# Two weight sums of a seven-product feed-forward step, moved from VectorE to accumulating DMA

## Chip, core and metric

The kernel runs on one core of a Trainium2 chip. The metric is the device time of one execution in microseconds (us); lower is better. Three runs of the kernel before gave 1428.53, 1428.57 and 1429.28 us, median 1428.57 us. A separate profiled execution gives the trace that is read below.

## What is computed

A two-layer hybrid block on 512 tokens of width 1024: layer 0 mixes tokens with dilated window attention, layer 1 with an mLSTM, and each is followed by a gated feed-forward block; a root-mean-square norm ends it. All data are 32-bit floats. Only the input half of the feed-forward block is changed:

```python
D_FF = -(-8 * D_MODEL // (3 * 256)) * 256        # 2816
def swiglu(xn, w_in, w_out):
    gu = xn @ w_in                                # 1024 x 5632
    return (jax.nn.silu(gu[..., :D_FF]) * gu[..., D_FF:]) @ w_out
```

The first 2816 columns of `gu` are called gates here, the last 2816 ups.

## The kernel before

Every matrix product is made of three TensorE passes: an operand is split into a rounded high part and the rest (`hi`, made by ScalarE on L208; `lo`, made by VectorE on L209), and high times high, high times low and low times high are summed in PSUM. `ffn_in` (L859) makes the hidden activations of a layer in pairs of 128 columns, j = 0, 2, ... 20. The pairs 0, 2 and 4 are made plainly (`plain`, L943). The eight pairs j = 6 to 20 are each made as one **step of seven products**: weights and tokens are seen as 2 x 2 blocks. A11 and A12 are the blocks of the gate columns for the upper and the lower 512 input features, A21 and A22 those of the up columns, each 512 x 256 numbers (512 KB, a tile of 128 x 1024). B11 to B22 are blocks of the normalized tokens. Sums of blocks are multiplied, seven products in place of eight (`PRODUCTS`, L855): p1 = A11 B11, p5 = S1 T1, p6 = S2 T2, p2 = A12 B21, p7 = S3 T3, p3 = S4 B22, p4 = A22 T4, in this order on TensorE.

The token sums T1 to T4 and their splits are made once a layer, while the plain pairs run (`normalized`, L893). The weight sums are made in every step, by VectorE on L988:

- S1 = A21 + A22, S2 = S1 - A11 (both in one tile, tag `t1`, of which there is one: the next step's S1 cannot be written before this step's S2 has been read for the last time, by S4);
- S3 = A11 - A21 (in place of A21, in the tile pair `w8`, of which there are two), S4 = A12 - S2 (in place of A12).

`weights_of` (L970) issues the four loads of a step on SyncE's queue (SP): A11 and A21 into one `w8` pair, A22 and A12 into tiles of the ring `wraw` (three). `prepare` (L992) splits one operand and then makes the sum that follows it; it runs two products ahead of TensorE (`AHEAD`, L857), because `hi` and `lo` are rings of three tiles (`W_BUFS`). So S1 of the next step is split while p4 of the present step runs, and S4 of the present step is made about when its p6 begins. `products` (L1005) issues the 24 matmuls of a product (L1017) and the evaluation: L1023 adds, L1055 the silu, L1056 and L1060 the products gate times up that give the two token halves of the hidden tile.

Each engine works through its instructions in program order; an engine that waits holds up all that is behind it. The loads of a step are issued as soon as their tile is free and the queue has come to them. GpSimd (POOL) issues no DMA in this stage of the kernel before.

Of the kernel before, what the change touches and what calls it, by code (L numbers as in the profile page):

```python
# [11 lines left out]
F32 = mybir.dt.float32  # L12
# [3 lines left out]
ALU = mybir.AluOpType  # L16
AX = mybir.AxisListType
P = 128
# [52 lines left out]
def tile_hybrid_dilated_attn_mlstm(  # L71
# [4 lines left out]
    nc = tc.nc  # L76
# [268 lines left out]
    with ExitStack() as actx:  # L345
# [16 lines left out]
        ang, n, sn, cs = (tmp[:, 0, i * P:(i + 1) * P] for i in range(4))  # L362
# [430 lines left out]
        def out_project(pairs, w2d, nk, name, first=0, end=KC // 2):  # L793
            for c in range(first, end):
# [4 lines left out]
        acc = [[acc_tile("awo0_%d" % m) for m in range(2)],  # L799
               [ps.tile([P, 512], F32, tag="s", name="awo1_%d" % m, bufs=2) for m in range(2)],  # L800
               [acc_tile("awo2_0"), ps.tile([P, 512], F32, tag="t", name="awo2_1", bufs=1)]]
# [51 lines left out]
    HALF = SEQ // 2  # L853
# [5 lines left out]
    def ffn_in(layer, fp, pair, rbc, hook, following):  # L859
# [4 lines left out]
        wi = ffn_w_in[layer]  # L864
# [20 lines left out]
        ops, raw = {}, {}  # L885
# [7 lines left out]
        def normalized():  # L893
            xs = [fp.tile([P, 4, SEQ], F32, tag="w8", name="f%dx%d" % (layer, i), bufs=2) for i in range(2)]
            for i in range(2):
                for t in range(2):
                    raw["B%d%d" % (i + 1, t + 1)] = xs[i][:, :, t * HALF:(t + 1) * HALF]
            for k in range(KC):
                nc.vector.scalar_tensor_tensor(xs[k // 4][:, k % 4], h[k], col("ffn", layer * KC + k), rbc,
                                               op0=ALU.mult, op1=ALU.mult)  # L900
                yield
            split_tokens("B11")
            raw["T1"] = fp.tile([P, 4, HALF], F32, tag="t1", name="f%dt1" % layer)
            nc.vector.tensor_tensor(raw["T1"], raw["B12"], raw["B11"], op=ALU.subtract)
            yield

            raw["T3"] = raw["B12"]
            nc.vector.tensor_tensor(raw["T3"], raw["B22"], raw["B12"], op=ALU.subtract)
            split_tokens("T1")
            yield  # L910
            split_tokens("T3")
            yield
            split_tokens("B22")
            yield
            raw["T2"] = raw["B22"]
            nc.vector.tensor_tensor(raw["T2"], raw["B22"], raw["T1"], op=ALU.subtract)
            split_tokens("T2")
            yield
            split_tokens("B21")
            yield  # L920

            raw["T4"] = raw["B21"]
            nc.vector.tensor_tensor(raw["T4"], raw["B21"], raw["T2"], op=ALU.subtract)
            split_tokens("T4")

        hid = []
# [43 lines left out]
        def weights_of(j):  # L970

            nm = "f%dj%d" % (layer, j)
            w8 = fp.tile([P, 2, 1024], F32, tag="w8", name=nm + "_w8", bufs=2)
            w = {"A11": w8[:, 0], "A21": w8[:, 1]}
            for key in ("A22", "A12"):
                w[key] = wp.tile([P, 1024], F32, tag="wraw", name=nm + key, bufs=W_BUFS)
            for key in ("A11", "A22", "A12", "A21"):
                half, ch = int(key[1]) - 1, int(key[2]) - 1
                c0 = half * D_FF + j * P
                nc.sync.dma_start(w[key].rearrange("p (k n) -> p k n", k=4),  # L980
                                  wi[ch * 4 * P:(ch + 1) * 4 * P, c0:c0 + 256].rearrange("(k p) n -> p k n", p=P))

            def split(key):
                return split_chunk((w[key], 1024, lambda t: t.rearrange("p (k n) -> p k n", k=4), nm + key))

            def total(key, a, b, op, place):
                w[key] = w[place]
                nc.vector.tensor_tensor(w[key], w[a], w[b], op=op)  # L988
            w["own"] = fp.tile([P, 1024], F32, tag="t1", name=nm + "S")
            made = {}  # L990

            def prepare(key):  # L992
                made[key] = split(key)

                if key == "A11":
                    total("S1", "A21", "A22", ALU.add, "own")
                elif key == "S1":
                    total("S2", "S1", "A11", ALU.subtract, "own")
                elif key == "S2":
                    total("S3", "A11", "A21", ALU.subtract, "A21")  # L1000
                elif key == "A12":
                    total("S4", "A12", "S2", ALU.subtract, "A12")
            return [(lambda key=key: prepare(key)) for key, _ in PRODUCTS], made

        def products(j, made):  # L1005
            nm = "f%dj%d" % (layer, j)
            acc, t = {}, {}
            first = lambda x: x.rearrange("p (m n) -> p m n", m=2)

            def product(key, okey, name, fresh=True):  # L1010
                if fresh:
                    acc[name] = bank("%s_%s" % (nm, name))
                whl = made[key]
                for m in range(2):
                    for k in range(4):
                        for a, b in SPLITS:
                            nc.tensor.matmul(acc[name][:, m * HALF:(m + 1) * HALF], whl[a][:, k, m * P:(m + 1) * P],  # L1017
                                             ops[okey][b][:, k],
                                             start=(fresh and m == 0 and k == 0 and (a, b) == SPLITS[0]),
                                             stop=(m == 1 and k == 3 and (a, b) == SPLITS[-1]), skip_group_check=True)  # L1020

            def add(out, x, y, op=ALU.add):
                nc.vector.tensor_tensor(out, x, y, op=op)  # L1023


            def p1():
                product("A11", "B11", "c11")
                acc["u"] = bank(nm + "_u")
                nc.scalar.activation(acc["u"], acc["c11"], AF.Copy)

            def p5():
                product("S1", "T1", "p5")
                t["v5"] = temp("v5", nm + "v5")
                nc.scalar.activation(t["v5"], acc["p5"], AF.Copy)

            def p6():
                product("S2", "T2", "u", fresh=False)
                t["u2"] = temp("u2", nm + "u2")
                nc.scalar.activation(t["u2"], acc["u"], AF.Copy)

            def p2():
                product("A12", "B21", "c11", fresh=False)
                t["g1"] = temp("gu0", nm + "g1", 3)
                nc.scalar.activation(t["g1"], acc["c11"], AF.Silu)

            def p7():
                product("S3", "T3", "u", fresh=False)
                add(t["v5"], acc["u"], t["v5"])

            def p3():  # L1050
                product("S4", "B22", "p5", fresh=False)
                hid.append(hidden(j // 2))
                t["g2"] = temp("gu0", nm + "g2", 3)
                add(t["g2"], acc["p5"], t["u2"])
                nc.scalar.activation(t["g2"], t["g2"], AF.Silu)  # L1055
                nc.vector.tensor_tensor(hid[-1][:, :, HALF:], first(t["v5"]), first(t["g2"]), op=ALU.mult)  # L1056

            def p4():
                product("A22", "T4", "u", fresh=False)
                nc.vector.tensor_tensor(hid[-1][:, :, :HALF], first(acc["u"]), first(t["g1"]), op=ALU.mult)  # L1060
            return [p1, p5, p6, p2, p7, p3, p4]

        split_next()
# [44 lines left out]
    with ExitStack() as fctx:  # L1108
        fp = pool(fctx, "ffn0")
        a, ready = ffn_in(0, fp, pair, rbc, hook,  # L1110
                          lambda ch: split_chunk(weight_chunk(ffn_w_out[0], ch, 0, 4, "fo0_k%d" % ch)))
# [17 lines left out]
    with ExitStack() as mctx:  # L1129
# [101 lines left out]
        for b in range(TB):  # L1231
            ve.scalar_tensor_tensor(fblk[32 * b:32 * b + H], blk(lf)[:, b], bias2[:, 1:2], blk(t0)[:, b],
                                    op0=ALU.add, op1=ALU.add)
# [174 lines left out]
    with ExitStack() as fctx:  # L1408
        fp = pool(fctx, "ffn1")
        wo = ffn_w_out[1]  # L1410

        def load(ch, n):
            src = wo[ch * 2 * P:(ch + 1) * 2 * P, n * 512:(n + 1) * 512].rearrange("(k p) n -> p k n", p=P)
            return split_weights(src, [P, 2, 512], "fw%d_%d" % (n, ch))
        a, ready = ffn_in(1, fp, pair, rbc, hook, lambda ch: load(ch, 0))
# [40 lines left out]
        for n in range(2):  # L1456
            acc = ([acc_tile("fin%d" % i) for i in range(3)] + [ps.tile([P, 512], F32, tag="t", name="fin3", bufs=1)]
                   if n == 0 else
                   [ps.tile([P, 512], F32, tag=tg, name="fin4", bufs=2) for tg in ("s", "s", "o", "o")]
                   + [acc_tile("fin5")])  # L1460
# [23 lines left out]
            for at, tb, cs in tiles:  # L1484
# [4 lines left out]
                t = ts[tb, n][:, cs]  # L1489
# [7 lines left out]
                if part == (1 if tb == TB - 1 else 0):  # L1497
                    nc.vector.tensor_tensor(fpre[:, tb:tb + 1], fss[:, tb, 0:1], fss[:, tb, 1:2], op=ALU.add)
                    nc.vector.tensor_scalar(fpre[:, tb:tb + 1], fpre[:, tb:tb + 1], 1.0 / D, EPS,
                                            op0=ALU.mult, op1=ALU.add)  # L1500
                nc.gpsimd.tensor_tensor(t, t, gbc[:, n * 512 + cs.start:n * 512 + cs.stop], op=ALU.mult)
                if n == 1 and cs.stop == 512:
# [3 lines left out]
                                                   op0=ALU.mult, op1=ALU.add)  # L1506
# [35 lines left out]
```

## Time and profile before

| what | value |
|---|---|
| median of three runs | 1428.57 us |
| the profiled execution, its own time | 1428.88 us |
| its span in the trace | 1427.1 us |
| TensorE (PE) busy | 1415.9 us, 99% |
| VectorE (DVE) busy | 960.4 us, 67% |
| ScalarE (ACT) busy | 603.4 us, 42% |
| seven-product stage, layer 0 | 571 to 732 us of the span |
| seven-product stage, layer 1 | 1139 to 1302 us of the span |
| packets of the SyncE queue | 125616, 131.55 MB, 29.6% of 16 DMA engines |
| packets of the GpSimd queue | 6320, 24.69 MB, 6.2% |

Times in the trace are counted from the start of the span. PE rows are matmuls, PEld rows weight loads beside them; SPq and POOL rows named DMA_DIRECT2D are the issuing of DMAs, whose landing is given apart. A number in brackets at the end of a row is the idle time of that engine before it, and what ended it.

### The profile page before, as it was taken

Reading aid. Unit: us, or ns where it says so; the run is one execution under the profiler, and the core shown is the slowest. Engines: PE = TensorE matmul, PEld = TensorE weight load, DVE = VectorE, ACT = ScalarE, POOL = GpSimd, SP = SyncE. Lnnn points to the kernel's source line nnn. Section 1 sums busy time; section 2 is a strip of 40 time slices with the busy share of each in tenths; the row PEclk is TensorE's granted clock in tenths of the full one; section 3 lists DMA queues with packets and bytes.
Section 4 is the critical chain, followed back from the end, with each engine's and each line's share of the span. In section 5 each row is a group of like instructions: output and inputs, shape, how many; then the busy total and the mean of one; then the engine's idle time right before and its main releaser. Section 6 shows DMA issues by size and latency. Waiting matters only on the chain. (4 is left out here: it accounts for less than half of the span.)

```text
span 1427.1 us, 20255 instructions
## 1 busy us (share of the span) xinstructions
PE 1415.9 (99%) x7986; PEld 1241.2 (87%) x7986; DVE 960.4 (67%) x1679; ACT 603.4 (42%) x1009; POOL 84.8 (6%) x137
## 2 busy tenths in 40 slices
PE   9999999999999999999999999999999999999998
PEld 7888888888888888999998888888888899998887
DVE  7857567567567397787782358897758777888233
ACT  5333224224225353444462233696534354445123
POOL 1011011011002000000000010110000000001001
PEclk9999999999999999999999999999999999999999
DMA  6346236235335434323233232321133332346331
GB/s 193 102 115 201 75 104 191 97 108 151 133 104 145 145 101 133 107 72 118 90 96 96 96 98 74 104 60 60 55 113 96 122 118 83 96 118 180 116 106 72
DMA packets 133688, 158.67 MB, mean 111 GB/s; under 512 B 7060, under 2 KB 121044, under 8 KB 133592
## 3 DMA queue, kind: packets, MB, share of 16 engines
q1 hardware_dynamic: 125616, 131.55, 29.6%
q0 software_dynamic: 6320, 24.69, 6.2%
q8 instruction: 63, 1.03, 0.3%
q10 hardware_dynamic: 1656, 1.12, 0.2%
q14 instruction: 33, 0.27, 0.1%
HBM read 143.18 MB, written 14.16 MB: 110 GB/s over the span
## 5 line engine op out<-in xcount | busy, mean ns | idle before, releaser
L1471 PE MATMUL fin<-fw_l,f1hh 128*128 128x512 f32 (+1 forms) x198 | 72.5, 366 | 0.0
L1471 PE MATMUL fin<-fw_h,f1hh 128*128 128x512 f32 (+1 forms) x198 | 72.4, 366 | 0.0
L1471 PE MATMUL fin<-fw_h,f1hl 128*128 128x512 f32 (+1 forms) x198 | 72.4, 365 | 0.0
L209 DVE TENSOR_TENSOR fo_k_l<-fo_k_w,fo_k_h 128x1024 fp32r<-128x1024 f32 (+1 forms) x24 | 27.2, 1135 | 62.0 <-ACT fo_k_h L208 62.0
L239 PE MATMUL fo<-f0hh,fo_k_h 128*128 128x512 f32 x176 | 68.5, 389 | 0.0
L239 PE MATMUL fo<-f0hl,fo_k_h 128*128 128x512 f32 x176 | 68.5, 389 | 0.0
L239 PE MATMUL fo<-f0hh,fo_k_l 128*128 128x512 f32 x176 | 68.5, 389 | 0.0
L209 DVE TENSOR_TENSOR fw_l<-fw_w,fw_h 128x1024 fp32r<-128x1024 f32 x22 | 27.1, 1233 | 59.9 <-ACT fw_h L208 59.9
L208 ACT ACTIVATE fo_k_h<-fo_k_w 128x1024 fp32r<-128x1024 f32 (+1 forms) x24 | 23.7, 989 | 74.7 <-PE fo L239 74.7
L208 ACT ACTIVATE fw_h<-fw_w 128x1024 fp32r<-128x1024 f32 x22 | 23.3, 1060 | 67.6 <-PE fin L1471 67.0
L1471 PEld LDWEIGHTS fin<-fw_l,f1hh 128*128 128x128 f32 x198 | 37.4, 189 | 6.2 <-DVE fw_l L209 0.2
L1471 PEld LDWEIGHTS fin<-fw_h,f1hh 128*128 128x128 f32 x198 | 37.3, 189 | 6.2
L1471 PEld LDWEIGHTS fin<-fw_h,f1hl 128*128 128x128 f32 x198 | 37.3, 188 | 6.0
L239 PEld LDWEIGHTS fo<-f0hh,fo_k_l 128*128 128x128 f32 x176 | 33.0, 188 | 6.9
L239 PEld LDWEIGHTS fo<-f0hl,fo_k_h 128*128 128x128 f32 x176 | 33.0, 188 | 6.9
L239 PEld LDWEIGHTS fo<-f0hh,fo_k_h 128*128 128x128 f32 x176 | 33.0, 188 | 6.7
L239 PE MATMUL f0j<-n_h,f0j_h 128*128 128x512 f32 x96 | 37.5, 390 | 0.0
L239 PE MATMUL f1j<-n_h,f1j_h 128*128 128x512 f32 x96 | 37.5, 390 | 0.0
L239 PE MATMUL f0j<-n_h,f0j_l 128*128 128x512 f32 x96 | 37.4, 389 | 0.0
L239 PE MATMUL f1j<-n_h,f1j_l 128*128 128x512 f32 x96 | 37.4, 389 | 0.0
L239 PE MATMUL f0j<-n_l,f0j_h 128*128 128x512 f32 x96 | 37.3, 389 | 0.0
L239 PE MATMUL f1j<-n_l,f1j_h 128*128 128x512 f32 x96 | 37.3, 389 | 0.0
(2105 smaller groups left out, 4886.0 us busy)
## 6 DMA issues: line engine op xcount, KB each, us to landing
f0j_w<-in_ffn_w_in_dram SPq DMA_DIRECT2D x28, 512.0 KB, 4.9
f1j_w<-in_ffn_w_in_dram SPq DMA_DIRECT2D x28, 512.0 KB, 4.4
fw_w<-in_ffn_w_out_dram SPq DMA_DIRECT2D x22, 512.0 KB, 3.9
fo_k_w<-in_ffn_w_out_dram SPq DMA_DIRECT2D x20, 512.0 KB, 3.5
awo_k_w<-in_attn_w_out_dram SPq DMA_DIRECT2D x8, 512.0 KB, 7.1
mv_k_w<-in_mlstm_w_in_dram SPq DMA_DIRECT2D x8, 512.0 KB, 3.7
mqk_k_w<-in_mlstm_w_in_dram SPq DMA_DIRECT2D x8, 512.0 KB, 3.9
mo_k_w<-in_mlstm_w_in_dram SPq DMA_DIRECT2D x8, 512.0 KB, 3.7
```

The lines of the kernel that those rows point to most:

```text
L208: nc.scalar.activation(hi[:, :n], raw[:, :n], AF.Copy)
L209: nc.vector.tensor_tensor(lo[:, :n], raw[:, :n], hi[:, :n].bitcast(F32), op=ALU.subtract)
L239: nc.tensor.matmul(acc, whl[a][:, k, m * P:(m + 1) * P], pairs[b][kk], start=(kk == 0 and (a, b) == SPLITS[0]), stop=(kk == nk - 1 and (a, ...
L1471: nc.tensor.matmul(acc[i][:, cs], a[a_][kk][:, tb * P:(tb + 1) * P], whl[b_][:, k, cs], start=(kk == 0 and (a_, b_) == SPLITS[0]), stop=(k ...
```

## The change

Signs are turned so that all four weight sums are additions: S1 = A21 + A22, S2 = S1 + A11, S3 = A11 + A21, S4 = A12 + S2. To fit, T1, T2 and T4 are negated, and the ups come out negated; the last multiplication of each half takes a factor -1. S1 and S3 are no longer made by VectorE: GpSimd's queue loads A21 into S1's tile and adds A22 onto it from DRAM by an accumulating DMA; SyncE's queue loads A11 a second time, into S3's tile, and GpSimd's queue adds A21 onto it. S2 and S4 stay on VectorE. A step then moves seven blocks in place of four.

```diff
-            nc.vector.tensor_tensor(raw["T1"], raw["B12"], raw["B11"], op=ALU.subtract)
+            nc.vector.tensor_tensor(raw["T1"], raw["B11"], raw["B12"], op=ALU.subtract)
-            nc.vector.tensor_tensor(raw["T2"], raw["B22"], raw["T1"], op=ALU.subtract)
+            nc.vector.scalar_tensor_tensor(raw["T2"], raw["T1"], -1.0, raw["B22"], op0=ALU.mult, op1=ALU.subtract)
-            nc.vector.tensor_tensor(raw["T4"], raw["B21"], raw["T2"], op=ALU.subtract)
+            nc.vector.scalar_tensor_tensor(raw["T4"], raw["T2"], -1.0, raw["B21"], op0=ALU.mult, op1=ALU.subtract)
...
-            w = {"A11": w8[:, 0], "A21": w8[:, 1]}
+            w = {"A11": w8[:, 0], "S3": w8[:, 1], "S1": fp.tile([P, 1024], F32, tag="t1", name=nm + "S")}
...
+            for key, block in (("A11", "A11"), ("S3", "A11"), ("A22", "A22"), ("A12", "A12")):
+                load(key, block, nc.sync)
+
+            load("S1", "A21", nc.gpsimd)
+            load("S1", "A22", nc.gpsimd, accum_op=ALU.add)
+            load("S3", "A21", nc.gpsimd, accum_op=ALU.add)
...
-                if key == "A11":
-                    total("S1", "A21", "A22", ALU.add, "own")
-                elif key == "S1":
-                    total("S2", "S1", "A11", ALU.subtract, "own")
-                elif key == "S2":
-                    total("S3", "A11", "A21", ALU.subtract, "A21")
+                if key == "S1":
+                    total("S2", "S1", "A11", "S1")
                 elif key == "A12":
-                    total("S4", "A12", "S2", ALU.subtract, "A12")
+                    total("S4", "A12", "S2", "A12")
...
-                nc.vector.tensor_tensor(hid[-1][:, :, HALF:], first(t["v5"]), first(t["g2"]), op=ALU.mult)
+                nc.vector.scalar_tensor_tensor(hid[-1][:, :, HALF:], first(t["v5"]), -1.0, first(t["g2"]),
+                                               op0=ALU.mult, op1=ALU.mult)
...
-                nc.vector.tensor_tensor(hid[-1][:, :, :HALF], first(acc["u"]), first(t["g1"]), op=ALU.mult)
+                nc.vector.scalar_tensor_tensor(hid[-1][:, :, :HALF], first(acc["u"]), -1.0, first(t["g1"]),
+                                               op0=ALU.mult, op1=ALU.mult)
```

More of the change, by code (lines that the diff above doesn't have):

```diff
@@ L973, in weights_of, with load, total @@
             w8 = fp.tile([P, 2, 1024], F32, tag="w8", name=nm + "_w8", bufs=2)
-            w = {"A11": w8[:, 0], "A21": w8[:, 1]}
+            w = {"A11": w8[:, 0], "S3": w8[:, 1], "S1": fp.tile([P, 1024], F32, tag="t1", name=nm + "S")}
             for key in ("A22", "A12"):
                 w[key] = wp.tile([P, 1024], F32, tag="wraw", name=nm + key, bufs=W_BUFS)
-            for key in ("A11", "A22", "A12", "A21"):
-                half, ch = int(key[1]) - 1, int(key[2]) - 1
+            def load(key, block, engine, **kw):
+                half, ch = int(block[1]) - 1, int(block[2]) - 1
                 c0 = half * D_FF + j * P
-                nc.sync.dma_start(w[key].rearrange("p (k n) -> p k n", k=4),
-                                  wi[ch * 4 * P:(ch + 1) * 4 * P, c0:c0 + 256].rearrange("(k p) n -> p k n", p=P))
+                engine.dma_start(w[key].rearrange("p (k n) -> p k n", k=4),
+                                 wi[ch * 4 * P:(ch + 1) * 4 * P, c0:c0 + 256].rearrange("(k p) n -> p k n", p=P), **kw)
+            for key, block in (("A11", "A11"), ("S3", "A11"), ("A22", "A22"), ("A12", "A12")):
[3 more added lines that the diff above has]
+            load("S3", "A21", nc.gpsimd, accum_op=ALU.add)
             def split(key):
                 return split_chunk((w[key], 1024, lambda t: t.rearrange("p (k n) -> p k n", k=4), nm + key))
-            def total(key, a, b, op, place):
+            def total(key, a, b, place):
                 w[key] = w[place]
-                nc.vector.tensor_tensor(w[key], w[a], w[b], op=op)
-            w["own"] = fp.tile([P, 1024], F32, tag="t1", name=nm + "S")
+                nc.vector.tensor_tensor(w[key], w[a], w[b], op=ALU.add)
             made = {}
```

## The prediction

> **What bounds the kernel now.** I read the page's busy times first, then who TensorE (PE) waits for, then one step of the changed stage on VectorE, ScalarE and PE.
>
> ```profile
> PE 1415.9 (99%) x7986; PEld 1241.2 (87%) x7986; DVE 960.4 (67%) x1679; ACT 603.4 (42%) x1009; POOL 84.8 (6%) x137
> ```
>
> PE is busy in all but 1427.1 - 1415.9 = 11.2 us of the span. The waits of PE:
>
> ```profile
> PE m1yT L305 <- ACT vaug L1169: 1.7, 1, 1.7
> PE idle L107 <- DVE idle_w L102: 1.5, 1, 1.5
> PE a0g0q L449 <- ACT first_h L439: 0.5, 1, 0.5
> PE m1nb L1312 <- ACT m0e L1322: 0.4, 1, 0.4
> PE xbc L329 <- DVE xdg L323: 0.3, 1, 0.3
> ```
>
> That is the whole list, and no line of the feed-forward stage is in it. In the timeline of PE the matmuls of L1017 start every 0.12 us without a gap from one product to the next: a product of 24 takes 2.88 us and a step of seven 20.16 us. So no VectorE instruction taken out of this stage can end it sooner; the change can gain nothing here, and what it costs depends on whether S1 and S3 are still ready in time. The step j = 14 on VectorE (start us, duration us):
>
> ```profile
> 649.34 1.23 DVE L209 TENSOR_TENSOR f0j14S_l<-f0j14S,f0j14S_h 128x1024 fp32r<-128x1024 f32 x1 [0.28 <-ACT f0j14S_h L208]
> 650.48 0.69 DVE L1056 TENSOR_TENSOR f0hid<-f0j12v,f0j12g 128x512 f32<-128x512 f32 x1
> 651.08 1.22 DVE L988 TENSOR_TENSOR f0j14S<-f0j14S,f0j_w 128x1024 f32<-128x1024 f32 x1
> ...
> 653.51 1.23 DVE L209 TENSOR_TENSOR f0j14S_l<-f0j14S,f0j14S_h 128x1024 fp32r<-128x1024 f32 x1 [0.61 <-ACT f0j14S_h L208]
> 655.15 1.23 DVE L209 TENSOR_TENSOR f0j14A_l<-f0j14A,f0j14A_h 128x1024 fp32r<-128x1024 f32 x1 [0.42 <-ACT f0j14A_h L208]
> 656.41 1.22 DVE L988 TENSOR_TENSOR f0j14A<-f0j14A,f0j14S 128x1024 f32<-128x1024 f32 x1
> 657.67 1.22 DVE L988 TENSOR_TENSOR f0j16S<-f0j_w,f0j16A 128x1024 f32<-128x1024 f32 x1
> ```
>
> The rows are: low part of S1, a hidden product, S2, low part of S2, low part of A12, S4, and at 657.67 already S1 of the *next* step. ScalarE first touches these two S1 here:
>
> ```profile
> 648.25 1.06 ACT L208 ACTIVATE f0j14S_h<-f0j14S 128x1024 fp32r<-128x1024 f32 x1 [1.82 <-PE f0j_p L1017]
> ...
> 668.41 1.06 ACT L208 ACTIVATE f0j16S_h<-f0j16S 128x1024 fp32r<-128x1024 f32 x1 [1.82 <-PE f0j_p L1017]
> ```
>
> And PE takes the low part of S2 first in p6, which starts here:
>
> ```profile
> 656.80 0.28 PE L1017 MATMUL f0j_u<-f0T2h,f0j14S_h 128*128 128x256 f32 x1
> ```
>
> Read together: the only S1 tile is free when S4 ends, 656.41 + 1.22 = 657.63, and S1 of j = 16 is wanted at 668.41, **10.78 us** later. VectorE needs 1.22 us of that; the change puts two DMAs one behind the other there. The low part of S2 is done at 654.74 and wanted at 656.80: S1 may come **2.06 us** late before PE stands (p5 has more room: 650.57 to its start at 653.92).
>
> **The change, part by part.**
>
> *Taken out:* two sums of 1.22 us in each of 16 steps, 39 us of VectorE. Worth nothing in time: PE has no gap that waits for them.
>
> *The factor -1:* `scalar_tensor_tensor` rows of 128x512 take 0.685 us (L1334, from PSUM) to 0.76 us (L227), against 0.69 us now on L1056 and L1060: 0 to 0.07 us for each of the two. T2 and T4 lie in the plain pairs, where VectorE has idle rows of 0.9 and 4.2 us. Nothing; without that cover some 0.1 us a step.
>
> *S3:* its tile is loaded a step ahead, its accumulate is issued when the second A11 has landed, and it is wanted only at p7. From the low part of S3 (ends about 659 with the sums gone) to the use two steps on there are some 38 us for a load and an accumulate. Hidden; the two would have to take over 30 us together. On GpSimd's queue the accumulate stands between two S1 pairs and waits for the second A11, which by the f0j_w row (4.9 us) lands some 6 us after S4; the S1 pair behind it is due only at the next S4, 20 us after.
>
> *SyncE's queue* still issues four loads a step (0.37 to 0.46 us each); both A11 are issued once the low part of S3 is made, about 1.3 us after S4, beside the A21 of the S1 chain.
>
> *S1, the new wait.* L is the time from the end of S4 to S1 complete. It is: GpSimd sees S4's end; plain load of A21; GpSimd sees it land; accumulate of A22; ScalarE sees it land.
> - The three hand-overs: an estimate of 0.1 us each, as sharp as the rows above follow one another: 0.3.
> - The plain load. Same shape, same queue, from DRAM: a0v (L677, 128x4x256, 512 KB), 0.78 us to issue and landed 4.2 us after its start, 4.3 to 4.6 in the three others. Those had the queue nearly alone. In this stage loads of 512 KB on the SyncE queue land after 4.9 us (median of f0j_w), f0j12A after 6.2. With two A11 loads beside it I take 5.2, between 4.2 and 6.2.
> - The accumulate is not in the trace. Lower bound: a plain load, 4.2, if the add and the reading of the old contents are free. It must fetch a second 512 KB, the tile itself, so the nearest row is a load of twice the bytes on the same queue: ht, 1 MB:
>
> ```profile
> DMA to landing us min/median/max: 6.1/6.8/7.6
> ```
>
> 960 KB (a0pT) took 6.7 to 9.3. Upper bound: reading and adding one after the other, 4.2 + 6.8 = 11. The A12 and A22 loads of SyncE's queue run beside it (issued 4.7 and 7.4 us after S4 now), so I take 7.5, the upper end of ht.
>
> L = 0.3 + 5.2 + 7.5 = **13.0 us**; bounds 8.7 and 17.5.
>
> What a late S1 does: from S1's first split to the end of S4 the rows take 657.63 - 648.25 = 9.38 us. Of this 0.50 is a wait of A12's split for PE (it could follow S2's low part after 1.14 and not 1.64 us), so the chain S1 to S4 can shrink to 8.88. Then a step cannot be shorter than L + 8.88, and PE's 20.16 holds only up to L = 11.28. With L = 13.0 the first transition is late by 13.0 - 10.78 = 2.2 us, each of the six that follow (j = 10 to 20) by 13.0 - 11.28 = 1.72 more: 12.5 us at j = 20, less the 2.06 of room = 10.5 us that PE stands, in each of two layers: **+21 us**. Each us of L beyond is 14 us. Behind the waiting split on ScalarE lies the silu of p3 (L1055), behind that on VectorE the hidden product L1056, S2 and L1060; they are in the 8.88 already. The first S1 of a layer is loaded while the plain pairs run (T1's last reader ends at 539.1, the split comes at 565) and is in time.
>
> Sum: 1428.9 (the profiled execution; 0.3 above the median of the runs) + 21 = 1450 us.
>
> The Trainium skill, "Collectives: The Full Stack", section "The bandwidth ceiling: the fold count and why AG ≠ RS ≠ AR", says that an adding DMA runs at about half the rate of a copy, since it reads two sources. By that, an estimate, the accumulate is the plain 4.2 us and once more the data time of 512 KB (32 rows an engine at 0.054 us on the SyncE queue, 1.7 us): 5.9 us, L = 11.4 and 1428.9 us; no row here shows it, and it leaves the two loads beside it out.
>
> **Rivals.**
> 1. *Hidden: no change.* The mechanism is the same chain with L up to 11.5: then the lateness (0.7 at first, 0.2 more each time, 2.0 at j = 20) stays within 2.06 and PE never stands: 1428.9. Against the 13.0 it needs a plain load at 4.6 and an accumulate at 6.6, which are the quiet values of a0v and ht; for it speaks that the DMA engines are only 0.32 to 0.36 busy in these windows. It decides from L = 11.5 down. The Trainium skill, "DMA: Bandwidth & Descriptors", section "Anatomy of one DMA — SWDGE (gpsimd) path", gives 2.0 us plus bytes over 436 GB/s for a DMA of GpSimd's queue: 3.2 us here, where the trace has 4.2 to 4.6, and 4.4 for two reads, so L = 7.9, an estimate, and this rival.
> 2. *Much slower accumulate.* If it passes 1 KB rows at a third or a quarter of the copy rate (0.054 us on the SyncE queue by the page: 0.296 x 16 x 1427 / 125616), the data alone take 32 x 0.16 to 0.22 = 5.2 to 6.9 us per engine, two of them and five copies fill 18.9 to 22.4 of 20.16 us, and all loads get slower. L = 16: 2 x (7 x 16 - 10.78 - 6 x 11.28 - 2.06) = 63, 1492 us.
> 3. *Faster.* Only if something that PE waits for goes; the list above holds 4.4 us, none in this stage. 1425 at best.
>
> **How the numbers follow.** Forecast (L from 11.7 to 15.2, 1432 to 1481 us) 0.54; hidden 0.28; much slower (over 1481) 0.14; faster 0.04. Two in a thousand, 2.9 us, is about what a measurement of this kernel can tell from no change; L = 11.7 gives it. So faster 0.04, same 0.28, slower 0.68. The range must take in the hidden case and leaves out the upper half of the slow one: 1427.5 to 1486, about 0.85 of the cases, as 0.28 lies in one point (the upper bound L = 17.5 would be 1513). Own range of the likeliest: 1432 to 1481.
>
> **What would show it.** Right: ScalarE's first split of S1 is ended by a DMA and not by PE; PE waits for S2's low part in p6 from about j = 10 on, little at first and then 1.7 us in each step; S1's split to S4's end takes 8.9 us; the accumulate lands about 7.5 us after its issue. Rival 1: S1's split is still ended by p3 and steps take 20.16. Rival 2: the DMA share of the stage goes from 0.34 to near 1. I would be wrong in kind if PE stood at p7 (S3) or behind a token product.

## The result, and the profile after

The changed kernel takes 1466.57 us (median of 4 runs, 1464.48 to 1470.31) against 1428.91: 1.0266 of the time before, interval 1.0243 to 1.029. It is slower by 37.7 us; 21 were forecast. Its profiled execution took 1465.22 us, with a span of 1463.4.

The busy times of the page after:

```profile
PE 1425.3 (97%) x7986; PEld 1244.4 (85%) x7986; DVE 922.3 (63%) x1647; ACT 600.9 (41%) x1009; POOL 138.5 (9%) x185
...
q0 software_dynamic: 25520, 49.86, 15.2%
```

VectorE has 38.1 us less to do, as the change means it to, GpSimd 53.7 more for 48 DMA issues, and its queue moves 25.17 MB more, 48 times 512 KB. PE does the same 7986 matmuls and is busy for 97% of a longer span: it now waits. (The page also counts 9.4 us more of busy time for the same matmuls, whose ends the profile models; the lateness is therefore read below from the starts of the products.) The first lines of its waits (us in total, times, longest) are all of the changed stage:

```profile
PE f1j_u L1018 <- ACT f1j_u L1030: 8.7, 6, 1.5
PE f0j_u L1018 <- ACT f0j_u L1030: 6.4, 6, 1.5
PE f0j_p L1018 <- ACT f0j10S_h L208: 1.7, 1, 1.7
```

`u` is the PSUM bank of p6: before PE may add S2 T2 to it, ScalarE copies p1 into it (L1030), and that copy stands in ScalarE's program behind the splits of S2 and A12, which wait for S1. What S1 waits for is seen in the step j = 14. S4 of j = 12 on VectorE, and GpSimd's issues:

```profile
644.65 1.23 DVE L994 TENSOR_TENSOR f0j12A<-f0j12A,f0j12S 128x1024 f32<-128x1024 f32 x1
...
646.42 0.78 POOL L980 DMA_DIRECT2D f0j14S<-in_ffn_w_in_dram  x1 [13.17 <-DVE f0j12A L994]
651.13 1.27 POOL L980 DMA_DIRECT2D f0j14S<-in_ffn_w_in_dram  x1 [3.92 <-DMA f0j14S<-in_ffn_w_in_dram]
```

The first issue waits for f0j12A on L994, which is this S4 (it ends at 645.88), the second for the landing of the first. Then ScalarE:

```profile
659.40 1.06 ACT L208 ACTIVATE f0j14S_h<-f0j14S 128x1024 fp32r<-128x1024 f32 x1 [5.82 <-DMA f0j14S<-in_ffn_w_in_dram]
...
665.48 0.58 ACT L1030 ACTIVATE f0j_u<-f0j_c 128x512 f32<-128x512 f32 x1
```

Before, this split was ended by p3 on PE; now it stands 5.82 us and a DMA ends it. From S4's end: hand-over to GpSimd 0.54, load 4.71, accumulate 8.27, together 13.52 us where there were 10.78. On VectorE the chain goes on, low part of S2, low part of A12, S4:

```profile
664.66 1.22 DVE L209 TENSOR_TENSOR f0j14S_l<-f0j14S,f0j14S_h 128x1024 fp32r<-128x1024 f32 x1 [0.61 <-ACT f0j14S_h L208]
665.81 1.22 DVE L209 TENSOR_TENSOR f0j14A_l<-f0j14A,f0j14A_h 128x1024 fp32r<-128x1024 f32 x1
667.06 1.23 DVE L994 TENSOR_TENSOR f0j14A<-f0j14A,f0j14S 128x1024 f32<-128x1024 f32 x1
```

S4 ends at 668.29, 8.89 us after S1's first split, and at 668.84 GpSimd issues the next load: the ring is closed, and this turn takes 13.52 + 8.89 = 22.4 us (22.8 in the mean of the 14 turns), where PE's step is 20.16. From the first product to the next stage layer 0 takes 178.9 us (161.3 before) and layer 1 180.4 (161.4), 36.7 us more in all, which is the whole difference of the two executions (36.3).

### The profile page after: what moved, and what is told of

The parts are those of the page before. It is cut to its first block, busy times and chain, and to the rows that moved or that the text cites. A ratio compares the mean times of both kernels' runs of the same rounds, so it can differ in the third digit from the quotient of the medians.

```text
span 1463.4 us, 20321 instructions
## 1 busy us (share of the span) xinstructions
PE 1425.3 (97%) x7986; PEld 1244.4 (85%) x7986; DVE 922.3 (63%) x1647; ACT 600.9 (41%) x1009; POOL 138.5 (9%) x185
```

## The experiments

Theory: the one tile of S1 puts a load and an accumulate one behind the other between S4 and the next S1, and this ring, not PE, sets the step. Rivals: the two accumulates and the doubled bytes cost by themselves; any two DMAs there are too long; S3's accumulate has its part.

**A second tile for S1.**

```diff
-            w = {"A11": w8[:, 0], "S3": w8[:, 1], "S1": fp.tile([P, 1024], F32, tag="t1", name=nm + "S")}
+            w = {"A11": w8[:, 0], "S3": w8[:, 1], "S1": fp.tile([P, 1024], F32, tag="s1", name=nm + "S", bufs=2)}
```

> The changed kernel with S1 in a tag of its own with two tiles, so that the two DMAs of S1 need not wait for the S4 of the step before; the same DMAs, the same sums. Theory (the one S1 tile puts load and accumulate between S4 and the next S1): S1 is there long before its split, ScalarE's split waits for p3 again, steps take 20.16 us, 1428 to 1431 us. Rival (the accumulates load the DMA engines or slow other work, whatever they wait for): at least half of the 38 us stays, 1448 us or more.

Measured: 1429.13 us, ratio 1.0 (0.999 to 1.0009). The whole loss is gone with the same DMAs. GpSimd still issues the two DMAs of S1 one behind the other, but those of j = 16 now follow S4 of j = 12, which ends at 637.52, a whole step earlier (the first row names a split of S3 that ended in between and does not touch this tile). ScalarE's split finds S1 done:

```profile
638.07 0.78 POOL L980 DMA_DIRECT2D f0j16S<-in_ffn_w_in_dram  x1 [9.57 <-ACT f0j12S_h L208]
643.12 1.28 POOL L980 DMA_DIRECT2D f0j16S<-in_ffn_w_in_dram  x1 [4.27 <-DMA f0j16S<-in_ffn_w_in_dram]
```

```profile
668.45 1.06 ACT L208 ACTIVATE f0j16S_h<-f0j16S 128x1024 fp32r<-128x1024 f32 x1 [1.82 <-PE f0j_p L1018]
```

The split is ended by p3 again, 25 us after the accumulate's issue. The DMA engines are 0.62 busy in this stage (0.30 before; the window line's last but one figure), and it costs nothing:

```profile
572.00:732.00 160.00, 160.00 (x1335) 159.96 (x1334) 112.05 (x108) 86.23 (x105) 20.02 (x18) 1.00 0.62 153
```

It also clears the factor -1 and the sign changes, which are all in this kernel.

**S1's sum back on VectorE, its tile and S3 left as changed.**

```diff
-            load("S1", "A22", nc.gpsimd, accum_op=ALU.add)
...
+                if key == "A11":
+                    total("S1", "S1", "A22", "S1")
```

> One tile for S1 as in the change, A21 loaded into it by GpSimd's queue, but A22 added by VectorE in place; S3 as in the change. Theory: the chain from S4 is 0.54 us hand-over, 4.8 us load and 1.3 us sum = 6.7 us, under the 10.78 there are: no stall, 1428 to 1431 us. It also says that S3's accumulate, though just as slow, is hidden. Rival (S3's accumulate and its traffic cost by themselves): 1440 us or more.

Measured: 1429.27 us, ratio 1.0001 (0.9991 to 1.0012). The single tile with one DMA behind S4 is harmless, the load lands after 4.0 to 4.6 us (5.3 once), and S3's accumulate, 6.7 to 7.8 us in the median of the two layers, costs nothing.

**S3's sum back on VectorE, S1 left as changed.**

```diff
-            for key, block in (("A11", "A11"), ("S3", "A11"), ("A22", "A22"), ("A12", "A12")):
+            for key, block in (("A11", "A11"), ("S3", "A21"), ("A22", "A22"), ("A12", "A12")):
...
-            load("S3", "A21", nc.gpsimd, accum_op=ALU.add)
...
+                elif key == "S2":
+                    total("S3", "A11", "S3", "S3")
```

> S1 by load and accumulate in one tile as in the change; S3 made by VectorE from A11 and A21 as before (six blocks moved in a step, not seven). Theory: S1's chain is nearly as long (13 to 13.9 us, as S3's accumulate stands behind it on the queue), so most of the loss stays: 1452 to 1466 us. Rival (both accumulates share the blame): about half, 1447 us.

Measured: 1467.06 us (2 runs), ratio 1.0266 (1.0245 to 1.0286), the full loss. S1's accumulate takes 8.7 us in the mean of the 14 transitions (from step to step of a layer), 8.4 in the changed kernel: S3's accumulate behind it does not lengthen it. With the run before this one, the loss is all S1's.

**S1's second DMA plain.** Same waits, but A22 overwrites A21.

```diff
-            load("S1", "A22", nc.gpsimd, accum_op=ALU.add)
+            load("S1", "A22", nc.gpsimd)
```

> The accumulate of S1 replaced by a plain load of A22 over A21 (A21 is left out of S1; S2 and S4 follow), the wait between the two DMAs kept. Theory: the accumulate's own time is what is too long; as a plain load it takes 4.8 to 5.5 us and not 8.4, the chain is 10.1 to 10.9 us, under 11.28: no stall, 1428 to 1432 us. Rival (any two DMAs in a row on GpSimd's queue are too long): 1440 us or more.

Measured: 1440.03 us (2 runs), ratio 1.0077 (1.0056 to 1.0097). The theory misses: most of the loss goes, but not all, and the time lies right at the rival's bound of 1440. So the rival, that two DMAs in a row are too long here, is partly right: it keeps about 11 of the 38 us, with L 12.05 in the mean and so above 11.28. The second plain load takes 5.8 to 7.8 us, 6.7 in the mean, and not 4.8 to 5.5; here j = 18:

```profile
684.05 0.77 POOL L980 DMA_DIRECT2D f0j18S<-in_ffn_w_in_dram  x1 [10.71 <-DVE f0j16A L994]
688.43 0.75 POOL L980 DMA_DIRECT2D f0j18S<-in_ffn_w_in_dram  x1 [3.61 <-DMA f0j18S<-in_ffn_w_in_dram]
```

```profile
695.93 1.06 ACT L208 ACTIVATE f0j18S_h<-f0j18S 128x1024 fp32r<-128x1024 f32 x1 [4.51 <-DMA f0j18S<-in_ffn_w_in_dram]
```

The first load takes 4.38 us to the issue behind it, the second is seen by ScalarE after 7.5. So adding costs 8.4 - 6.7 = 1.7 us in this place, and something else lengthens whatever DMA comes second. The next two runs ask whether that is the loads of A12 and A22, which SyncE issues just then.

**The prices by themselves.** The kernel before, with 24 DMAs in a row, each waiting for the one before, during the first output product, where SyncE's queue issues a load of 512 KB every 4 to 5 us:

```diff
+        for i in range(3):
+            nc.gpsimd.dma_start(view(4), rows1(0, 4))
+            nc.gpsimd.dma_start(view(4), rows1(1, 4))
+            nc.gpsimd.dma_start(view(4), rows1(0, 4), accum_op=ALU.add)
+            nc.gpsimd.dma_start(view(4), rows1(1, 4), accum_op=ALU.add)
+            nc.gpsimd.dma_start(pr, rows4(i))
+            nc.gpsimd.dma_start(pr, rows4(i + 3), accum_op=ALU.add)
...
```

> The kernel before, with 24 extra DMAs on GpSimd's queue into an unused tile while the first feed-forward output product runs, each waiting for the one before: plain and accumulating, 512 KB in 1 KB rows, 512 KB in 4 KB rows, 256 KB in 1 KB rows. It prices the accumulate with little beside it. Theory: a plain 512 KB lands after 4.1 to 4.5 us also when it follows another at once, the accumulate after 5.8 to 6.2 (once more 32 rows at 0.054 us an engine), so that the rest of the 8.4 us comes from the loads beside it. Rival: the accumulate takes 7.5 us or more also alone. The time of the kernel, 1428 to 1431 us, says nothing here.

The issues on GpSimd (L1118 and L1119 plain, L1120 and L1121 accumulating, all 512 KB in 1 KB rows; L1122 plain and L1123 accumulating in 4 KB rows); from one start to the next is a DMA with its hand-over:

```profile
718.63 0.76 POOL L1118 DMA_DIRECT2D probe<-in_ffn_w_in_dram  x1 [252.42 <-ACT f0j20S_h L208]
722.92 0.76 POOL L1119 DMA_DIRECT2D probe<-in_ffn_w_in_dram  x1 [3.52 <-DMA probe<-in_ffn_w_in_dram]
727.34 1.33 POOL L1120 DMA_DIRECT2D probe<-in_ffn_w_in_dram  x1 [3.66 <-DMA probe<-in_ffn_w_in_dram]
737.65 1.29 POOL L1121 DMA_DIRECT2D probe<-in_ffn_w_in_dram  x1 [8.98 <-DMA probe<-in_ffn_w_in_dram]
743.73 0.57 POOL L1122 DMA_DIRECT2D probe<-in_ffn_w_out_dram  x1 [4.79 <-DMA probe<-in_ffn_w_in_dram]
747.71 0.86 POOL L1123 DMA_DIRECT2D probe<-in_ffn_w_out_dram  x1 [3.41 <-DMA probe<-in_ffn_w_out_dram]
753.23 0.74 POOL L1124 DMA_DIRECT2D probe<-in_ffn_w_in_dram  x1 [4.66 <-DMA probe<-in_ffn_w_out_dram]
```

Plain 4.29 and 4.42 us here, and 4.16 to 5.87 over the three rounds, with a mean of 4.8; the second of two takes 4.42, 4.16 and 5.06, the first 4.29, 5.87 and 5.08, so a plain load right behind another is not slow in itself. Accumulating it is 10.31, 6.05, 6.81 (L1120) and 6.08, 9.13, 6.62 (L1121), with a mean of 7.5. The two shortest agree with the estimate, plain and once more the data time, 1.7 us more; the mean lies at the rival's 7.5. One execution with such a spread does not decide between them. In 4 KB rows it is 3.98 to 5.42 plain and 5.52 to 7.22 accumulating.

The trace's records of single DMA packets show more. In the 4 KB rows a typical packet takes 159 ns plain and 328 ns accumulating (medians, L1122 and L1123). That is also what the Trainium skill says ("Collectives: The Full Stack", "The bandwidth ceiling: the fold count and why AG ≠ RS ≠ AR": an adding DMA reads two sources), and the trace agrees: twice the time for a packet. In the 1 KB rows the 1.7 us are made up of two parts: in the 6.08 us accumulate the first packet moves 0.5 us later than in the 4.29 us load (1.99 against 1.50 us after the issue), and the data take 1.4 us longer (3.45 against 2.04). Why two of the six took 9.1 and 10.3 us is not explained by this run.

**A12 and A22 behind the accumulate.** Their loads go to GpSimd's queue, where they are issued after S1's accumulate.

```diff
-            for key, block in (("A11", "A11"), ("S3", "A11"), ("A22", "A22"), ("A12", "A12")):
+            for key, block in (("A11", "A11"), ("S3", "A11")):
...
+            for key, block in (("A22", "A22"), ("A12", "A12")):
+                load(key, block, nc.gpsimd)
```

> The changed kernel with the loads of A12 and A22 issued on GpSimd's queue, behind S1's accumulate, in place of SyncE's queue beside it; same bytes, same sums, one S1 tile. Theory (S1's accumulate is lengthened from 6 to 8.4 us by the loads beside it): it lands after 6 to 7 us, the chain is 11.3 to 12.3 us, 1429 to 1446 us. Rival (the accumulate is 8.4 us whatever lies beside it): chain of 13.8 us, 1460 to 1468 us.

Measured: 1439.57 us (1434.16 to 1444.17, 3 runs), ratio 1.0069 (1.0044 to 1.0093). The profiled execution is the fastest of the three, 1434.16. In it the accumulate takes 5.8 to 8.3 us, 6.6 in the mean, and the chain from S4 to S1 11.6 instead of 13.9. The step j = 14:

```profile
639.54 0.76 POOL L980 DMA_DIRECT2D f0j14S<-in_ffn_w_in_dram  x1 [10.29 <-DVE f0j12A L996]
643.97 1.31 POOL L980 DMA_DIRECT2D f0j14S<-in_ffn_w_in_dram  x1 [3.67 <-DMA f0j14S<-in_ffn_w_in_dram]
644.75 1.30 POOL L980 DMA_DIRECT2D f0j14A<-in_ffn_w_in_dram  x1
```

A12 (f0j14A) is issued right behind S1's accumulate, which here takes 5.92 us: close to the shortest of the run above. So of the 8.4 us about 1.8 come from the two loads beside it, and the same bytes cost less when they queue up behind. The packet records say how: the first packet of S1's accumulate moves 2.02 to 2.04 us after its issue in all 14 transitions here, and 1.98 to 4.12 in the changed kernel, with a mean of 3.2. So 1.2 of the 1.8 us are a later start. The time and the chain are in the theory's range; the rival is out. What is left of the loss fits an L that is still above 11.28.

**Is VectorE's relief worth anything?** In these steps it can't be, PE has no gap to give. VectorE is fullest while it makes the token sums; with PLAIN = 4 a pair more is made by seven products, and the first step comes 21 us earlier, on their heels (in the kernel before with PLAIN = 4 VectorE is busy for 23.4 of the 24 us before it). The edit is the one number, in the kernel before and in the one with two S1 tiles.

> The kernel before with PLAIN = 4: the pair j = 4 is also made as a step of seven products. A plain pair is 96 matmuls of 0.226 us = 21.7 us, a step 20.16, so at most 1.6 us a layer can be won, 3.1 in all. VectorE must then have the token sums and the first S1 and S3 ready some 21 us earlier, when it has no free time: I expect a stall of 2 to 6 us at the first step of each layer, 1428 to 1438 us.

> The changed kernel with two S1 tiles and PLAIN = 4. If VectorE's relief is worth something anywhere it is at the first step after the token sums, where VectorE is full: two sums of 1.22 us fewer. Against it, S1's load and accumulate (11 us) can start only when their tiles are free. Theory that the relief pays: faster than the kernel before with PLAIN = 4 by 2 to 5 us in all. Rival (the two DMAs take what VectorE gives): same or slower than it.

Measured: the kernel before with PLAIN = 4 takes 1429.13 us, ratio 0.9999 (0.999 to 1.0008): inside the expected range, but nothing won. Its first step loses 1.2 us in layer 0 and 1.3 in layer 1, less than the 2 to 6 expected. The changed kernel with two S1 tiles and PLAIN = 4 takes 1427.38 us (11 runs, 1426.73 to 1428.11), ratio 0.9987 (0.9978 to 0.9996) to the kernel before. It is the fastest of all, by 0.1%: less than the 0.2% that the prediction set as measurable, but its interval lies below 1. Against the kernel before with PLAIN = 4 it is 1.75 us faster, just under the 2 to 5 that were expected. The timeline shows where a part of it lies: with VectorE's sums PE's matmuls have gaps around p6 and p2 of the first step in both layers (0.72 us the largest), with the DMA sums there is none in layer 0 and one of 1.21 us in layer 1. The stage of layer 0 is 1.2 us shorter by this, of 2.1 between the two profiled executions. That the two sums taken off VectorE are the reason, and not the sums' place in its program, was not tried apart.

## The prediction, point by point

- *PE has no gap, so nothing can be won in the stage:* right. The second tile gives back the time before (ratio 1.0, 0.999 to 1.0009), with 36 us less on VectorE.
- *The ring S4, hand-over, load, hand-over, accumulate, S1, S4 sets the step:* right, and shown by the second tile and by the sum put back on VectorE. S1's split to S4's end was forecast at 8.88 us and is 8.88 to 8.89 in all 14 transitions.
- *The size of L:* the step that was mis-sized. The terms, means of the 14 transitions:

| term | forecast | measured |
|---|---|---|
| S4's end to the load's issue | 0.1 | 0.64 (about 0.55 in eleven) |
| load of A21, with its hand-over | 5.2 + 0.1 | 4.9 |
| accumulate, with its hand-over | 7.5 + 0.1 | 8.4 |
| L | 13.0 | 13.9 |

With the sums of the measured L (97.0 and 98.0 us over seven transitions) the prediction's formula gives 97.0 - 10.77 - 6 x 11.28 - 2.06 = 16.5 and 17.5, together 34.0, against 36.7 measured: 0.9 us of L accounts for 13 of the 16 us by which the forecast was short, as the factor 14 said. It was luck that L was not further off: the load was taken 0.4 us too long, the hand-over 0.5 too short. The hand-over could have been priced better from the profile of before: VectorE's a1pB ended at 232.94 and GpSimd's issue behind it began at 233.24, 0.30 us. The accumulate's excess lies in the two loads beside it: with A12's and A22's loads moved behind, it takes 6.6 us, where I took 6.8, and they add 1.8, where I put 0.7.
- *Where PE stands:* nearly right. It stands at p5, for S1's split or its low part, and at p6; but at p6 not for the low part of S2: in the step j = 14 ScalarE's copy of p1 into the bank ends 0.18 us later (666.06 against 665.88). I had listed what is queued behind S1's split on ScalarE only up to the silu. The larger part of the 2.7 us that the formula misses is a place that it did not have. In the last step of each layer PE stands once more at p4, in layer 1 at p3 too, by 0.9 us more than before in layer 0 and 1.25 in layer 1:

```profile
PE f1j_u L1018 <- ACT f1hh L1088: 0.7, 1, 0.7
PE f0j_u L1018 <- DVE f0j20v L1024: 0.6, 1, 0.6
```

  f0j20v is VectorE's addition that reads the bank of p7 (L1024); in both layers it stands in VectorE's program among the splits for the next stage, and PE goes on in p4 0.14 to 0.15 us after it ends, though the profile puts the wait of layer 1 down to ScalarE's split f1hh. About 0.6 us stays unexplained, in which the 0.18 us of the copy have a part.
- *S3 hidden:* right; with S3 on VectorE the full loss stays.
- *The factor -1 at nothing:* right; the second-tile kernel has it.
- *Rival 1 (hidden, L up to 11.5):* wrong here, but it was near: with A12 and A22 out of the way L is 11.6. The estimate of L = 7.9 that the prediction gives beside it falls: a plain load of 512 KB on GpSimd's queue takes about 4 us or more in every run here, not 3.2.
- *Rival 2 (accumulate at a third or a quarter of the copy rate):* wrong; an accumulating packet of 1 KB takes 0.102 us (median), about twice the 0.054 us of the SyncE queue, not three or four times as long. The stage's DMA share is 0.58 to 0.62, not near 1.

## What to carry to other kernels

Before an operation is moved from an engine to DMA, look for what its destination tile waits for: the time from the tile's release to its first reader, not the transfer's bandwidth, is the budget, and here two DMAs one behind the other did not fit where one 1.2 us instruction did. A second tile was the remedy, and it cost only memory. A lateness in such a ring adds up step by step, so 1 us of a latency that is misjudged was worth 14 us here; and relieving an engine pays only where the bounding engine waits for it.

## What the hardware showed that was not expected

An accumulating DMA of 512 KB in 1 KB rows on GpSimd's queue took 6.05 us at best and 7.5 in the mean of six, a plain one 4.16 at best and 4.8 in the mean, with light traffic beside them. The issue itself takes 1.27 to 1.33 us on GpSimd against 0.76 to 0.79, and 0.86 to 0.90 against 0.57 when the rows are 4 KB. In the packet records the plain load moves these 1 KB rows as 128 packets of 4 KB, the accumulating one as 512 packets of 1 KB. Beside two 512 KB loads of another queue the same accumulate took 8.4 us and a plain load 6.7, while behind it on its own queue those loads lengthened it to only 6.6. From VectorE's last write to GpSimd's DMA issue about 0.55 us passed in eleven of 14 transitions.
